# Attention with corner masks by a TensorE product, and small per-row steps on GpSimd

## The chip, the cores and the metric

The kernel runs on one core of a Trainium2 chip. A core has five engines, each with its own instruction queue that is worked off in order: PE (TensorE, matrix products), DVE (VectorE), ACT (ScalarE), POOL (GpSimd) and SP (SyncE, which only issues DMAs here). They wait for one another through semaphores. Products land in PSUM, eight banks of 128 partitions x 2 KB; everything else lies in SBUF. POOL does not read PSUM in this kernel. The metric is the device time of one execution in microseconds.

## The reference

One layer of a streaming encoder, 1024 positions, width 1024. Two groups of 8 heads attend side by side: MLA heads (96 columns for queries and keys, causal in chunks of 64 positions) and band heads (64 columns, each chunk of 64 sees itself and 8 chunks before it, with a bias by relative position). Then one output projection and a gated MLP with a short convolution.

```python
CHUNK = 64; LEFT_CHUNKS = 8; Q_BLOCK = 128
...
q = rmsnorm(q, g_mla_q[l])          # over 96 columns, the 32 rotary ones among them
k = rmsnorm(k, g_mla_k[l])
q = concat([q[..., :NOPE], rope(q[..., NOPE:], positions)])
k = concat([k[..., :NOPE], rope(k[..., NOPE:], positions)])
...
# MLA: blocks of 128 queries
mask = key_chunk[None, :] <= q_chunk[:, None]
p = softmax(where(mask, (q @ k.T) * scale, -1e30))
o_mla = p @ v
...
# band: chunk ci of 64 queries against 576 keys
s = (q @ k.T) * scale + bias
p = softmax(where(kj >= (LEFT_CHUNKS - ci) * CHUNK, s, -1e30))
o_ca = p @ v
...
x = x + g_a * (concat([o_mla, o_ca]) @ w_out)
x = x + g_m * (silu(conv(h @ w_up)[gate]) * conv(h @ w_up)[val]) @ w_down
```

The blocks of 128 queries hold two chunks of 64. In an MLA block, the first 64 queries must not see the last 64 keys: one corner of 64x64 on the diagonal. In a band block from the fifth on, the last 64 queries must not see the first 64 keys: one corner at the other end. The kernel keeps scores negated, so a masked score is +1e30 and the softmax takes a row minimum.

## The kernel before

Values are float32, split into a high and a low part, so that a product is three products on PE (high by high, high by low, low by high). The program is written in Python, and a scheduler with a timeline of its own decides the order of instructions on each engine, by priorities that the code sets and by a few fixed orders (`issue_after`).

The stages, in order of time. First the modulation vectors and the first projections. Then the attention loop at lines 974 to 989: 128 score tiles, 16 units of 4 tiles for the band heads and 16 units of 4 for the MLA heads, in this order. A unit is one head and one half of the queries; a tile is one block of 128 queries. Between the tiles the loop places pieces of other work for PE, the "fillers" (line 924): projections of the next heads (`f_qk`, `f_v`), the latent projection (`f_m`), the MLA up-projections (`f_up`) and the band half of the output projection (`f_oca`). Last come the output projection, the gated MLP and the down-projection, which the change does not touch.

A tile passes through `Unit.scores` (line 735). PE computes its scores into `s`, one of two score areas of 1024 columns in PSUM: line 758 for band tiles, with a stationary page `qh` that holds the query's high part and then `ql` with its low part, line 764 for MLA tiles. DVE writes 1e30 into the 64x64 corner (line 771 for band tiles with `i >= 4`, line 782 for every MLA tile), then takes the row minimum `m` (lines 775 and 779 with the bias, or 783). ACT computes the exponential into `pr` and the row sum `rsum` (line 790), which frees the score area. DVE takes the reciprocal `ri` of the row sum (792) and multiplies it by the constant 2^15 (793). POOL scales the probabilities to a float16 high part (line 73, called at 809), DVE writes the low part (812), and SP issues a transposing DMA (824). The transposed probabilities meet the values on PE three tiles later (`Unit.values`, line 852), and the result is stored by SP (866).

In `f_up` (line 591) each block of 128 positions gives queries and keys of four MLA heads. DVE sums squares (632, 641), adds the sum over the shared rotary part, `ssr`, to the four key sums (642), and POOL makes the reciprocal roots from these (`rsqrt_mean`, lines 117 and 118). DVE then normalises and rotates (648 to 654, with `rope_apply` at 460 to 463). Line 84 is the helper with which POOL or DVE makes the low half of a weight, and line 718 a copy of a query page on POOL.

In tile names, `sc`, `mc`, `Pc`, `hlc`, `ric`, `PTc`, `pvc` belong to band tiles and `sm`, `mm`, `Pm`, `hlm`, `rim`, `PTm`, `pvm` to MLA tiles.

Of the kernel before, what the change touches and what calls it, by code (L numbers as in the profile page):

```python
# [16 lines left out]
BF16 = mybir.dt.bfloat16  # L17
# [7 lines left out]
P = 128  # L25
# [7 lines left out]
BIG = 1e30  # L33
# [31 lines left out]
def layer_kernel(ctx, tc, I, out):  # L65
# [6 lines left out]
    def scale_pool(o, i, s):  # L72
        pool.tensor_scalar(o, i, s, 1.0, op0=MUL, op1=MUL)  # L73
# [25 lines left out]
    make_identity(nc, ident)  # L99
    ones = cst.tile([P, P], F32, name="ones")  # L100
    pool.memset(ones[:], 1.0)
    nhalf = cst.tile([P, 1], F32, name="nhalf")
    pool.memset(nhalf[:], -0.5)
    modT = cst.tile([P, 4, ND], F32, name="modT")
# [486 lines left out]
    def f_up(gr):  # L591
        if gr == 0:
            right.__exit__(None, None, None)
            for i in "4v3":
                G["cm" + i] = tc.tile_pool(name="gp" + i, bufs=1, side="right", reuse_waits="tile")
                G[i] = G["cm" + i].__enter__()
        wq = []
        for k in range(2):
            raw = qtile(f"wqr{gr}_{k}")
            sp.dma_start(raw[:, :384], I["w_qu"][gr][:, k, :])  # L600
            w = g4([P, 2, 512], F32R, f"wq{gr}_{k}")
            hi_of("a", w[:, 0, :384], raw[:, :384])
            lo_of("p", w[:, 1, :384], raw[:, :384], w[:, 0, :384])
            wq.append(w)
        raw = qtile(f"wkr{gr}")
        sp.dma_start(raw[:], I["w_kvu"][gr])
        ssw = cst.tile([P, 1], F32, name=f"sswm{gr}")
        junk = qtile(f"wkj{gr}")
        act.activation(junk[:, 0:256].rearrange("p (a b) -> p a b", a=4),
                       raw[:].rearrange("p (a b) -> p a b", a=4)[:, :, NOPE:], AF.Square, accum_out=ssw[:])  # L610
        vscale["m", gr] = pow2_scale(f"m{gr}", ssw[:], gb2[:], 1, float(KVR))
        sc = vscale["m", gr][0]
        wk = g4([P, 2, 512], F32R, f"wk{gr}")
        hi_of("a", wk[:, 0], raw[:])
        lo_of("p", wk[:, 1], raw[:], wk[:, 0])
        for t in range(NT):
            h, j = divmod(t, 4)
            sl = slice(j * P, (j + 1) * P)
            if t % 2 == 0:
                mq[gr, t // 2] = g3([P, 2, 4, QK], F32, f"qn{gr}_{t}")  # L620
                mk[gr, t // 2] = g3([P, 2, 4, QK], F32, f"kn{gr}_{t}")
                mv[gr, t // 2] = G["v"].tile([P, 2, 4, 2, 64], F16, name=f"vt{gr}_{t}", tag="Gv", bufs=8)
            pt = ps.tile([P, 512], F32, name=f"qu{gr}_{t}", tag="mm", bufs=2)
            yield from gemm3_f(pt[:, :384], [(latT[k, h][:, 0, sl], latT[k, h][:, 1, sl], wq[k][:, 0, :384], wq[k][:, 1, :384])
                                for k in range(2)])
            rq = rtile(f"uqr{gr}_{t}")
            act.activation(rq[:, :384], pt[:, :384], AF.Copy)
            sq = qtile(f"usq{gr}_{t}")
            act.activation(sq[:, :384], rq[:, :384], AF.Square)
            ss = cst.tile([P, 8], F32, name=f"uss{gr}_{t}", tag="ss", bufs=4)  # L630
            r = cst.tile([P, 8], F32, name=f"ur{gr}_{t}", tag="rr", bufs=4)
            dve.tensor_reduce(ss[:, 0:4], sq[:, :384].rearrange("p (a b) -> p a b", a=4), axis=AX.X, op=ADD)
            pt = ps.tile([P, 512], F32, name=f"ku{gr}_{t}", tag="mm", bufs=2)
            yield from gemm3_f(pt[:], [(latT[2, h][:, 0, sl], latT[2, h][:, 1, sl], wk[:, 0], wk[:, 1])])
            p4 = pt[:].rearrange("p (a b) -> p a b", a=4)
            raw = rtile(f"kraw{gr}_{t}")
            r3 = raw[:, :256].rearrange("p (a b) -> p a b", a=4)
            act.activation(r3, p4[:, :, 0:NOPE], AF.Copy)
            s3 = raw[:, 256:512].rearrange("p (a b) -> p a b", a=4)
            act.activation(s3, r3, AF.Square)  # L640
            dve.tensor_reduce(ss[:, 4:8], s3, axis=AX.X, op=ADD)
            dve.tensor_tensor(ss[:, 4:8], ss[:, 4:8], ssr[:, t:t + 1].to_broadcast([P, 4]), op=ADD)
            rsqrt_mean(r[:], ss[:], QK)
            v_t = mv[gr, t // 2][:, t % 2]
            act.activation(v_t[:, :, 0, :], p4[:, :, NOPE:], AF.Copy, scale=sc)
            dve.scalar_tensor_tensor(v_t[:, :, 1, :], p4[:, :, NOPE:], sc, v_t[:, :, 0, :], op0=MUL, op1=SUB)
            q_t = mq[gr, t // 2][:, t % 2]
            dve.tensor_tensor(q_t, rq[:, :384].rearrange("p (a b) -> p a b", a=4),
                              r[:, 0:4].unsqueeze(2).to_broadcast([P, 4, QK]), op=MUL)
            rope_apply(q_t[:, :, NOPE:], q_t[:, :, NOPE:], tabq, t, 4, rq[:, 0:256], dve)  # L650
            k_t = mk[gr, t // 2][:, t % 2]
            dve.tensor_tensor(k_t[:, :, 0:NOPE], r3, r[:, 4:8].unsqueeze(2).to_broadcast([P, 4, NOPE]), op=MUL)
            dve.tensor_tensor(k_t[:, :, NOPE:], kr[:, t:t + 1, :].to_broadcast([P, 4, ROPE]),
                              r[:, 4:8].unsqueeze(2).to_broadcast([P, 4, ROPE]), op=MUL)
# [72 lines left out]
    class Unit:  # L727
# [7 lines left out]
        def scores(u, i):  # L735
# [8 lines left out]
            with tc.high_priority(offset=OFF_S):  # L744
                s = ps.tile([P, 1024], F32, name=f"s{nm}", tag="S", bufs=2)
                n0 = max(0, min(4, i + 1) - lo) * P
                n1 = n - n0
                c0 = 512 - n0 if n1 else 0
                segs = [(c0, lo * P, n0, 0)] if n0 else []
                if n1:  # L750
                    segs.append((512, max(lo, 4) * P - 512, n1, 1))
                q = slice((i % 4) * P, (i % 4 + 1) * P)
                rs_ = slice(u.base, u.base + u.rows)
                if u.band:
                    qh, ql = qpg
                    for a, rr in ((qh[u.odd], slice(0, P)), (ql, rs_)):
                        for c, ko, w, kh in segs:
                            last = pe.matmul(s[:, c:c + w], a[rr, q], kpgs[kh][rr, u.odd, ko:ko + w],
                                             start=(a is not ql), stop=(a is ql))
                else:  # L760
                    for a in range(2):
                        for c, ko, w, kh in segs:
                            for b in range(2 - a):
                                last = pe.matmul(s[:, c:c + w], qpg[a][rs_, q], kpgs[kh][rs_, b, ko:ko + w],  # L764
                                                 start=(a == 0 and b == 0), stop=(a == 1))
                trail.append(last.ins)
                sv = s[:, c0:c0 + n]
                m = cst.tile([P, 1], F32, name=f"m{nm}", tag="m", bufs=4)
                if u.band:
                    if i >= 4:  # L770
                        dve.memset(sv[64:128, 0:64], BIG)
                    w = min(n, 256)
                    if n > 256:
                        m0 = cst.tile([P, 1], F32, name=f"m0{nm}", tag="m0", bufs=4)
                        dve.tensor_reduce(m0[:], sv[:, :n - 256], axis=AX.X, op=MIN)
                        init = m0[:]
                    else:
                        init = 3e38
                    anchor["dve"] = dve.tensor_tensor_reduce(sv[:, n - w:n], sv[:, n - w:n], bias[:, 256 - w:256], 1.0, init,  # L779
                                             ADD, MIN, accum_out=m[:]).ins  # L780
                else:
                    dve.memset(sv[0:64, n - 64:n], BIG)
                    anchor["dve"] = dve.tensor_reduce(m[:], sv, axis=AX.X, op=MIN).ins  # L783
                short = n <= (640 if u.band else 512)
                pieces = [(0, n)] if short else [(0, 512), (512, n)]
                if n <= 640:
                    pr = at.tile([P, 640], F32, name=f"P{nm}", tag="P", bufs=P_BUFS)
                else:
                    pr = pgtile([P, 1024], F32, f"P{nm}")
                act.activation(pr[:, :n], sv, AF.Exp, bias=m[:], scale=-1.0, accum_out=rsum[:, 0:1])  # L790
            with tc.high_priority(offset=OFF_P):
                dve.reciprocal(ri[:], rsum[:, 0:1])
                dve.tensor_scalar(ri[:], ri[:], PSCALE, None, op0=MUL)  # L793
                for x, (p0, p1) in enumerate(pieces):
                    w = p1 - p0
                    cnt[0] += 1
# [773 lines left out]
```

## Time and profile before

| | us |
|---|---|
| runs of the kernel before, median of 3 | 1380.44 (1379.88 to 1385.12) |
| the profiled execution, own time | 1379.88 |
| its span, first to last instruction | 1378.1 |
| first and last start of band score products (line 758) | 92.8 to 377.3 |
| first and last start of MLA score products (line 764) | 413.8 to 633.0 |
| last product of probabilities and values (line 852), start | 647.1 |
| first product of the MLP (line 1068), start | 734.6 |
| mean granted clock of PE | 0.940 |

How to read the views that follow. In a view of stretches each engine's column gives its busy microseconds and, in brackets, its instructions; then come the clock granted to PE (1 is full), the mean busy share of the DMA engines, and GB/s. In a list of waits, "A L1 <- B L2: t, n, m" says that A's instructions of line 1 began late because of B's of line 2, t us in total, n times, m us at most. A group of instructions has its line, engine and operation, output and input tiles with their shapes, its count, busy us, the mean of one in ns, and the idle time before it. A line of one source gives shortest/median/longest in ns. A timeline starts with the start and the duration in us. Instructions on one engine overlap a little in the records, so that durations add up to more than the time from start to start.

### The profile page before, as it was taken

What the parts mean: (1) busy time and instruction counts of PE and PEld (TensorE: products, weight loads), DVE (VectorE), ACT (ScalarE), POOL (GpSimd) and SP (SyncE); (2) the same over time, 40 slices, a digit from 0 to 9 for tenths busy, and PEclk for the clock granted to TensorE, in tenths of its full rate; (3) what the DMA queues carried; (4) which work ended last, traced back from release to release, by engine and by line L of the source; (5) the groups of instructions that cost most, each with busy time, mean ns of one, the idle gap of its engine ahead of it and who ended that gap; (6) DMA issues with size and microseconds to landing.
All of it is one profiled execution on the core that took longest, in us unless ns stands there. A gap on an engine that the chain in (4) does not pass through costs nothing.

```text
span 1378.1 us, 18696 instructions
## 1 busy us (share of the span) xinstructions
PE 1229.5 (89%) x6168; PEld 1009.3 (73%) x6168; DVE 1105.8 (80%) x1928; ACT 622.0 (45%) x1131; POOL 572.2 (42%) x610
## 2 busy tenths in 40 slices
PE   4889698989867779886997999999999999999998
PEld 3788487977655567674775888777788888888886
DVE  6957878676589997885689689898988888688667
ACT  4443445444455554554365443434444444443341
POOL 5454556365646574343643443434444442200000
PEclk9999797999787989997998999999999999999999
DMA  8314557666322468678921233333323224983451
GB/s 321 129 41 91 135 144 189 157 137 146 64 50 74 81 141 183 136 136 204 376 101 46 87 128 104 121 128 116 109 92 113 92 100 142 340 308 119 130 161 61
DMA packets 223689, 190.57 MB, mean 138 GB/s; under 512 B 148708, under 2 KB 166884, under 8 KB 223592
## 3 DMA queue, kind: packets, MB, share of 16 engines
q1 hardware_dynamic: 223592, 189.38, 47.5%
q8 instruction: 48, 0.79, 0.2%
q14 instruction: 49, 0.40, 0.1%
HBM read 117.24 MB, written 37.49 MB: 112 GB/s over the span
## 4 chain that ended last, share of the span: by engine, by line
PE 44%; DVE 16%; issue 5%; ACT 4%; DMA 4%; POOL 2%; SPq 0%; ACTq 0%; DVEq 0%; POOLq 0%
PE p L1068 6%; PE p L1070 6%; PE p L1069 6%; PE dnA_P L1381 2%; PE dnA_P L1383 2%; PE dnA_P L1382 2%; PE sm L764 2%; DVE u L1235 2%; PE dnB_P L1383 1%; PE dnB_P L1381 1%; PE dnB_P L1382 1%; DMA adaw<-w_ada 1%; DVE hlm L812 1%; DVE u L1234 1%; PE pvm L852 1%
## 5 line engine op out<-in xcount | busy, mean ns | idle before, releaser
L77 ACT ACTIVATE dnP<-dnr 128x1024 fp32r<-128x1024 f32 x73 | 77.4, 1062 | 113.1 <-PE dnA_P L1383 46.4
L1355 DVE TENSOR_TENSOR dnP<-dnr,dnP 128x1024 fp32r<-128x1024 f32 x72 | 89.5, 1246 | 46.5 <-ACT dnP L77 46.5
L73 POOL TENSOR_SCALAR hlm<-Pm,rim 128x512 f16<-128x512 f32 (+3 forms) x96 | 66.6, 702 | 75.8 <-ACT Pm L790 21.2
L1234 DVE SCALAR_TENSOR_TENSOR u<-c,cvp,u 128x1023 f32<-128x1023 f32 x44 | 62.0, 1449 | 29.6 <-ACT u L1233 29.6
L84 POOL TENSOR_TENSOR wf<-wu,wf 128x512 fp32r<-128x512 f32 x22 | 35.8, 1628 | 118.5 <-ACT wf L77 118.5
L73 POOL TENSOR_SCALAR hlc<-Pc,ric 128x640 f16<-128x640 f32 (+2 forms) x64 | 47.4, 744 | 72.2 <-DVE ric L793 40.6
L812 DVE SCALAR_TENSOR_TENSOR hlm<-Pm,rim,hlm 128x512 f16<-128x512 f32 (+3 forms) x96 | 67.7, 714 | 8.8 <-POOL hlm L73 8.4
L790 ACT ACTIVATE Pm<-sm,mm 128x128 f32<-128x128 f32 (+3 forms) x64 | 47.2, 738 | 52.5 <-DVE mm L783 31.8
L84 POOL TENSOR_TENSOR wb<-wu,wb 128x512 fp32r<-128x512 f32 x22 | 38.8, 1763 | 73.1 <-ACT wb L77 72.1
L1233 ACT ACTIVATE u<-c,cvp 128x1024 f32<-128x1024 f32 x44 | 52.3, 1237 | 34.4 <-DVE c L1304 25.8
L1235 DVE SCALAR_TENSOR_TENSOR u<-c,cvp,u 128x1022 f32<-128x1022 f32 x44 | 64.8, 1512 | 0.0
L852 PE MATMUL pvm<-PTm,vt 128*128 128x256 f16 (+1 forms) x320 | 45.9, 295 | 20.9 <-DMA PTm<-hlm 13.9
L790 ACT ACTIVATE Pc<-sc,mc 128x640 f32<-128x640 f32 (+2 forms) x64 | 42.0, 657 | 48.5 <-DVE mc L779 35.8
L812 DVE SCALAR_TENSOR_TENSOR hlc<-Pc,ric,hlc 128x640 f16<-128x640 f32 (+2 forms) x64 | 53.5, 840 | 12.7 <-POOL hlc L73 12.5
L852 PEld LDWEIGHTS <-vt 128*128 128x128 f16 x320 | 31.9, 109 | 35.7 <-DMA PTm<-hlm 14.4
L154 PE MATMUL ipq<-wq_s,hT 128*128 128x256 f32 x192 | 55.9, 294 | 1.2 <-ACT wq_s L77 1.2
L155 PE MATMUL ipq<-wq_s,hT 128*128 128x256 f32 x192 | 56.4, 294 | 0.1
L156 PE MATMUL ipq<-wq_s,hT 128*128 128x256 f32 x192 | 56.0, 292 | 0.0
L77 ACT ACTIVATE wc<-ws 128x512 fp32r<-128x512 f32 x21 | 13.3, 632 | 93.6 <-DVE ws L1087 93.6
L1382 PE MATMUL dnA_P<-dnP 128*128 128x512 f32 x132 | 51.3, 389 | 0.0
L1383 PE MATMUL dnA_P<-dnP 128*128 128x512 f32 x132 | 51.3, 389 | 0.0
L1381 PE MATMUL dnA_P<-dnP 128*128 128x512 f32 x132 | 51.2, 389 | 0.0
(432 smaller groups left out, 4453.4 us busy)
## 6 DMA issues: line engine op xcount, KB each, us to landing
wu<-w_up SPq DMA_DIRECT2D x44, 512.0 KB, 3.8
dnr<-g_d SPq DMA_DIRECT2D x73, 256.0 KB, 4.4
aw<-w_ada SPq DMA_DIRECT2D x48, 256.0 KB, 3.5
g_d<-u SPq DMA_DIRECT2D x22, 512.0 KB, 2.8
dnr<-w_down SPq DMA_DIRECT2D x44, 256.0 KB, 5.6
adaw<-w_ada_a SPq DMA_DIRECT2D x16, 512.0 KB, 6.1
x<-x SPq DMA_DIRECT2D x16, 512.0 KB, 9.0
g_d<-gs SPq DMA_DIRECT2D x22, 256.0 KB, 2.2
```

What stands on the lines that cost most here:

```text
L73: pool.tensor_scalar(o, i, s, 1.0, op0=MUL, op1=MUL)
L77: act.activation(o, i, AF.Copy)
L790: act.activation(pr[:, :n], sv, AF.Exp, bias=m[:], scale=-1.0, accum_out=rsum[:, 0:1])
L812: dve.scalar_tensor_tensor(hl[:, w:2 * w], pp, ri[:], hl[:, :w], op0=MUL, op1=SUB)
L852: last = pe.matmul(dst, u.vst(j), mov, start=(x == 0), stop=(x == len(todo) - 1), skip_group_check=True)
L1068: pe.matmul(pt, sh, pg[:, 0], start=(k == 0 and not add), stop=False, skip_group_check=skip)
L1069: pe.matmul(pt, sh, pg[:, 1], start=False, stop=False, skip_group_check=skip)
L1235: dve.scalar_tensor_tensor(u[:, 2:], c[:, :S - 2], cvp[:, cv:cv + 1], u[:, 2:], op0=MUL, op1=ADD)
L1355: r = f(*a, **k)
L1381: pe.matmul(pt, sh, w[:, 0, 0], start=start, stop=False, skip_group_check=add)
L1382: pe.matmul(pt, sh, w[:, 1, 0], start=False, stop=False, skip_group_check=add)
L1383: pe.matmul(pt, sl, w[:, 0, 0], start=False, stop=stop, skip_group_check=add)
```

## The change

Three edits. The corner masks are no longer written by DVE: between the products with the high and the low part of the queries, PE adds a product of one row. Its stationary is one partition of a constant tile, 64 zeros and 64 times 1e30 (or the reverse), its moving operand 64 ones, and its output the 64 columns of the corner on all 128 queries, so that 1e30 is added to 64 queries and zero to the others. The multiplication of the reciprocal row sums by 2^15 goes from DVE to POOL, by the helper that POOL uses for the probabilities. The addition of the rotary sums of squares to the key sums goes from DVE to POOL. Two constant tiles are made by POOL at the start.

```diff
+    mones = cst.tile([P, 64], BF16, name="mones")
+    pool.memset(mones[:], 1.0)
+    mrow = cst.tile([P, 3, 64], BF16, name="mrow")
+    pool.memset(mrow[:], 0.0)
+    pool.memset(mrow[:, 1], BIG)
+    mflat = mrow[:].rearrange("p a b -> p (a b)")
...
-            dve.tensor_tensor(ss[:, 4:8], ss[:, 4:8], ssr[:, t:t + 1].to_broadcast([P, 4]), op=ADD)
+            pool.tensor_tensor(ss[:, 4:8], ss[:, 4:8], ssr[:, t:t + 1].to_broadcast([P, 4]), op=ADD)
...
                     for a, rr in ((qh[u.odd], slice(0, P)), (ql, rs_)):
+                        if i >= 4 and a is ql:
+                            pe.matmul(s[:, c0:c0 + 64], mflat[0:1, 0:P], mones[0:1], start=False, stop=False,
+                                      skip_group_check=True)
                         for c, ko, w, kh in segs:
...
                     for a in range(2):
+                        if a:
+                            e = segs[-1][0] + segs[-1][2]
+                            pe.matmul(s[:, e - 64:e], mflat[0:1, 64:64 + P], mones[0:1], start=False, stop=False,
+                                      skip_group_check=True)
                         for c, ko, w, kh in segs:
...
-                    if i >= 4:
-                        dve.memset(sv[64:128, 0:64], BIG)
...
-                    dve.memset(sv[0:64, n - 64:n], BIG)
...
                 dve.reciprocal(ri[:], rsum[:, 0:1])
-                dve.tensor_scalar(ri[:], ri[:], PSCALE, None, op0=MUL)
+                scale_pool(ri[:], ri[:], PSCALE)
```

The helper that it calls stood in the kernel before:

```python
    def scale_pool(o, i, s):
        pool.tensor_scalar(o, i, s, 1.0, op0=MUL, op1=MUL)
```

The scheduler lays out the attention stages anew with these instructions; from the early part of the MLP on the order is that of before.

## The prediction

> **What bounds the kernel now.** I read the page's engine line first, then the stretches of the span, then the waits, then single lines.
>
> ```profile
> span 1378.1 us, 18696 instructions
> PE 1229.5 (89%) x6168; PEld 1009.3 (73%) x6168; DVE 1105.8 (80%) x1928; ACT 622.0 (45%) x1131; POOL 572.2 (42%) x610
> ```
>
> PE is the busiest engine of the whole span, but that is an average over stages. The change touches only instructions that run between the first score product and the last softmax, so the next view cuts the span there: band attention (92 to 392 us), the MLA up-projection (392 to 416), MLA attention beside the second up-projection (416 to 500), MLA attention beside part of the output projection (500 to 640), and the rest.
>
> ```profile
> core 0: us, PE busy (x) PEld busy (x) DVE busy (x) ACT busy (x) POOL busy (x), PEclk, DMA share, GB/s
> 92.00:392.00 300.00, 264.17 (x1634) 222.88 (x1635) 220.29 (x613) 136.42 (x348) 159.84 (x233) 0.89 0.56 128
> 392.00:416.00 24.00, 16.36 (x77) 11.38 (x74) 21.11 (x68) 14.55 (x34) 11.56 (x11) 1.00 0.06 15
> 416.00:500.00 84.00, 59.88 (x273) 46.30 (x274) 77.93 (x231) 46.98 (x112) 57.55 (x58) 0.76 0.41 93
> 500.00:640.00 140.00, 122.15 (x693) 96.93 (x693) 116.23 (x285) 69.68 (x146) 61.44 (x83) 0.96 0.74 150
> 640.00:1378.00 738.00, 703.64 (x3067) 574.24 (x3065) 601.24 (x597) 313.60 (x420) 228.91 (x160) 0.97 0.41 144
> ```
>
> Dividing busy by length: in the band stage PE leads (88%, DVE 73%); from 392 to 500 DVE leads (21.11+77.93 of 108, 92%, PE 71%); from 500 to 640 the two are level (PE 87%, DVE 83%). POOL is nowhere above 69%. So the change, which moves work from DVE to PE and POOL, meets three different limits. Which wait ends last there:
>
> ```profile
> POOL hlc L73 <- DVE ric L793: 40.6, 13, 7.5
> ACT Pm L790 <- DVE mm L783: 31.8, 17, 4.2
> POOL uss L117 <- DVE uss L642: 29.7, 11, 5.2
> POOL hlm L73 <- DVE rim L793: 12.0, 8, 2.7
>   ACT Pm L790: 24.4, 24
> ```
>
> The columns are total us, times, longest. The last row is of line 764: PE stood idle 24.4 us before MLA score products until an exponential had emptied one of the two score banks. The exponential itself waits for DVE's row minimum (L783), and POOL's probability scaling (L73) waits for DVE's scaled reciprocal (L793). The loop is PE scores, DVE minimum, ACT exponential, PE scores; DVE's queue is what is late in it.
>
> **What is removed.** Counting instructions in the program: 32+64 memsets of a 64x64 corner (L771, L782), 128 one-column scalings (L793), 16 four-column additions (L642); 240 DVE instructions.
>
> ```profile
> L771 DVE MEMSET sc<- x32: 112/112/112, 124.4 to 378.1; 64x64 f32 x32
> L782 DVE MEMSET sm<- x64: 112/112/112, 416.1 to 633.5; 64x64 f32 x64
> L793 DVE TENSOR_SCALAR rim<-rim x64: 125/142/155, 418.0 to 637.8; 128x1 f32<-128x1 f32 x64
> ```
>
> By stretch (us busy, count), first L782, then L793, then L642:
>
> ```profile
> 416.00:500.00 84.00, 2.20 (x20) 0.76 0.41 93
> 500.00:640.00 140.00, 4.89 (x44) 0.96 0.74 150
> ...
> 92.00:392.00 300.00, 9.22 (x64) 0.89 0.56 128
> 416.00:500.00 84.00, 2.65 (x19) 0.76 0.41 93
> 500.00:640.00 140.00, 6.55 (x45) 0.96 0.74 150
> ...
> 392.00:416.00 24.00, 0.86 (x6) 1.00 0.06 15
> 416.00:500.00 84.00, 1.76 (x10) 0.76 0.41 93
> ```
>
> From 392 to 500, where DVE leads, 2.20+2.65+0.86+1.76 = 7.5 us leave its queue; I count all of it. From 500 to 640, 4.89+6.55 = 11.4 us leave; PE is just as full, so I count half, 5.7. In the band stage 32x0.112+9.22 = 12.8 us leave an engine that is not the limit; I count nothing, and would count a third (4.3) if DVE set the pace there too. Bounds: 0 and the whole 31.7.
>
> **What PE gets.** 96 products of a one-row stationary (128 columns, bf16) with 64 moving columns, each with a weight load, put between the high and the low score products. No row shows such a product. The nearest is eight load-and-multiply pairs with one moving column:
>
> ```profile
> 270.28 0.95 PE L436 MATMUL p_ada<-ones,aacc 128*128 128x1 f32 x8
> 271.09 0.36 PE L154 MATMUL ipq<-wq_s,hT 128*128 128x256 f32 x1
> ```
>
> Eight pairs take 271.09-270.28 = 0.81 us, 0.10 each; a short product cannot cover the load that follows it, so the pair costs a load whatever its width. I take 0.10 (bounds 0, if the loads hide behind the 512-column products beside it, and 0.20, if the next load is bared as well). Band: 32x0.10 = 3.2 us on the leading engine, counted whole. 416 to 500: 20x0.10 = 2.0 us beside a fuller DVE, counted as nothing; without that cover it is 2.0. 500 to 640: 44x0.10 = 4.4, half counted, 2.2. The product reads only constants, so it adds no wait; what is queued behind it is the low product that ends the tile. The memset's 0.112 us between scores and minimum goes, PE's 0.10 comes, so a tile's own latency stays.
>
> **What POOL gets.** 128 one-column scalings, 16 four-column additions, three memsets at the start. Nearest rows:
>
> ```profile
> L483 POOL TENSOR_SCALAR mss<-mss 128x1 f32<-128x1 f32 x8 | 2.1, 267 | 0.7
> L117 POOL TENSOR_SCALAR uss<-uss 128x8 f32<-128x8 f32 x16 | 5.7, 353 | 30.8 <-DVE uss L642 29.7 <-DVE rim L793 0.8
> L118 POOL TENSOR_TENSOR rx<-ssx,nhalf x8: 549/549/868, 12.8 to 23.2; 128x1 f32<-128x1 f32 x8
> ```
>
> A scaling is taken at 0.27 us: 128x0.27 = 34.6 us on an engine that is busy 159.84+11.56+57.55+61.44 = 290.4 of the 548 us from 92 to 640. The additions lie inside the 29.7 us for which POOL waited for DVE's addition; with the cover gone they cost 16x0.35 = 5.6. POOL's first use of a sum is at 12.8 us, after its start-up memsets. The handover of one tile, with DVE's queue empty and with something in it:
>
> ```profile
> 582.53 0.17 DVE L792 RECIPROCAL rim<-rsm 128x1 f32<-128x1 f32 x1
> 582.73 0.15 DVE L793 TENSOR_SCALAR rim<-rim 128x1 f32<-128x1 f32 x1
> 583.04 1.04 POOL L73 TENSOR_SCALAR hlm<-Pm,rim 128x512 f16<-128x512 f32 x2 [3.30 <-ACT Pm L790]
> ...
> 576.22 0.16 DVE L792 RECIPROCAL rim<-rsm 128x1 f32<-128x1 f32 x1
> 576.30 0.67 DVE L783 TENSOR_REDUCE mm<-sm 128x1 f32<-128x512 f32 x1
> 576.89 0.14 DVE L793 TENSOR_SCALAR rim<-rim 128x1 f32<-128x1 f32 x1
> 577.28 0.59 POOL L73 TENSOR_SCALAR hlm<-Pm,rim 128x384 f16<-128x384 f32 x1 [0.43 <-DVE rim L793]
> ```
>
> From the reciprocal's start to POOL's first work on the probabilities: 0.51 us and 1.06 us. With the scaling on POOL it would be 0.17 + a handover of 0.16 (582.88 to 583.04) + 0.27 = 0.60. So a tile that met a queue gains 0.46 and one that did not loses 0.09. POOL waited for the scaling in 13+8 = 21 tiles of 128: 21x0.46 = 9.7 gained, 107x0.09 = 9.6 lost. I take 0 (bounds -9.7 and 128x0.09 = +11.5). The new wait is POOL's for the reciprocal. In the changed order 75 of the 128 scalings stand directly ahead of their own tile's L73; behind the other 53 stand low halves of weights (L84), query copies (L718) and powers (L118), which PE's fillers, the score products and the next norms wait for.
>
> POOL's additional instructions can also hold up DVE:
>
> ```profile
> 427.71 2.62 POOL L84 TENSOR_TENSOR wo<-wor,wo 128x512 fp32r<-128x512 f32 x2
> 428.02 1.17 DVE L462 TENSOR_TENSOR qn<-uqr 128x64 f32<-128x64 f32 x1
> 429.12 1.29 DVE L463 TENSOR_TENSOR qn<-uqr 128x64 f32<-128x64 f32 x1
> ...
> L462 DVE TENSOR_TENSOR qn<-uqr 128x64 f32<-128x64 f32 x1 | 0.2, 203 | 0.0
> L812 DVE SCALAR_TENSOR_TENSOR hlm<-Pm,rim,hlm 128x512 f16<-128x512 f32 (+3 forms) x96 | 67.7, 714 | 8.8 <-POOL hlm L73 8.4
> ```
>
> A DVE subtraction of two SBUF tiles that takes 0.203 us alone took 1.17 and 1.29 beside two POOL subtractions. L812 is such an instruction and fills 67.7 of 224 us, 30%. A 0.27 us scaling that falls on one holds it for 0.13 us on average: 64x0.30x0.13 = 2.5 us in the MLA stages and less in the band stage; I take 2 (bounds 0 and 144x0.27 = 39). The Trainium skill, "SBUF — State Buffer", section "Who interferes with whom", says more: VectorE with two SBUF inputs and a GpSimd instruction that reads SBUF exclude each other, and the later one is blocked for the other's whole length. The 1.29 us row agrees. By that rule each POOL scaling is bought with its full length whenever it meets such an instruction, which is the first rival.
>
> **The sum.** -7.5 -5.7 +2.2 +3.2 +0 +2 = -5.8 us, against the profiled execution's own 1379.88 us (span 1378.1 and 1.8 around it): 1374.1, so 1374. The median of the three runs, 1380.44, lies 0.6 above that execution, within what runs differ by.
>
> One thing is in no term: instructions are laid out anew. Outside the longest common order, 897 of PE's 6739 instructions, 418 of DVE's 1691 that remain, 166 of 956 on ACT, 89 of 616 on POOL and 101 of 685 on SP stand elsewhere, most of them in the attention stages and the last early in the MLP; on SP that puts probability transposes and stores of attention outputs ahead of or behind loads of weights. It can go either way by several us, and widens the range by 6.
>
> **Rivals.**
> *POOL's scalings hold DVE* (slower). For: the row of 1.29 us, and L812 following each scaling closely. Against: the scaling is short, and DVE's minima (0.67 us at 576.30) read a score bank and only one operand. Price: every scaling and addition blocks DVE for 0.27 us. From 392 to 500, (19+16)x0.27 = 9.5 whole; from 500 to 640, 45x0.27 = 12.2, half, 6.1. In place of the 2 that gives -5.8-2+15.6 = +7.8: 1388. It decides from the point where the average block exceeds what the scaling freed, 0.14 us. The skill's page on SBUF, named above, states this rival's rule.
> *DVE sets the pace throughout* (larger gain). For: the first four rows of the waits. Against: 88% PE in the band stage. -7.5-11.4-4.3, PE only in the band stage, +3.2: -20, 1360.
> *The change frees nothing that counts.* The loop waits on transposes of the probabilities and on score banks, and DVE only idles longer. Against: 92% from 392 to 500. Then only the additions' 0.86+1.76 gain and PE's 3.2 are paid: 1380.5.
>
> **How the numbers follow.** Forecast 0.40 (own range 1368 to 1380, half of it below 1373.5), larger gain 0.22 (1360), nothing 0.10 (1380.5), POOL holds DVE 0.28 (1388). A measurement of this kernel can tell about 0.5%, 6.9 us, from no change. Faster: 0.20+0.22 = 0.42; within: 0.20+0.10 = 0.30; slower: 0.28. Range: 1360, the larger gain, to 1394, the slower rival with the 6 of the new order.
>
> **What would show it.** DVE busy down by about 30 us, all between 92 and 640; POOL up by about 35 to 40. L73's waits for the reciprocal well under the 40.6+12.0 of before. The mask products 0.1 us apart from their neighbours, PE's busy time up by 10 to 20. The stretch from 392 to the last softmax shorter by some 9 us, the band stage longer by 3; after it both programs alike. Wrong if L812 and L648 grow in mean by more than 0.1 us (first rival), if the band stage moves by more than 8 us either way (the new order), or if a mask product takes 0.2 us or more.

## The result and the profile after

| | us |
|---|---|
| changed kernel, median of 16 runs | 1387.01 (1379.06 to 1394.89) |
| kernel before, median of 16 runs beside them | 1379.70 (1374.86 to 1385.12) |
| ratio, 95% interval | 1.0055 (1.0035 to 1.0074) |
| profiled execution of the changed kernel, own time | 1393.37, span 1391.6 |

The change makes the kernel slower by about 7.6 us. 1374 and a gain were forecast: the time lies inside the range, the direction was wrong. The profiled execution took 6.4 us more than the median, so its stretches are to be read for shape and not to the microsecond. The engine line of the page after:

```profile
span 1391.6 us, 18773 instructions
PE 1260.4 (91%) x6264; PEld 1026.4 (74%) x6264; DVE 1086.8 (78%) x1688; ACT 621.3 (45%) x1131; POOL 615.3 (44%) x757
```

DVE lost 240 instructions but only 19.0 us of busy time, POOL gained 43.1 us and PE 30.9. The stretches, cut near the same events as before (first band score, last band values, first MLA score, start of the output projection's pieces, 7 us ahead of the last MLA values); the columns are those of before:

```profile
95.80:396.30 300.50, 268.34 (x1661) 227.98 (x1662) 207.31 (x511) 134.76 (x344) 175.38 (x295) 0.89 0.56 128
396.30:421.00 24.70, 16.58 (x74) 12.63 (x72) 21.21 (x63) 15.44 (x37) 13.94 (x19) 0.93 0.05 14
421.00:510.40 89.40, 75.75 (x330) 55.05 (x329) 82.11 (x197) 50.06 (x118) 69.13 (x96) 0.74 0.45 100
510.40:655.50 145.10, 133.34 (x718) 99.33 (x715) 102.55 (x187) 69.07 (x144) 73.10 (x119) 0.94 0.68 143
```

The band stage is as long as before (300.5 us). In the last stretch PE is now at 133.34/145.1 = 92% and DVE at 71%, where 87% and 83% stood before: the two are no longer level. The waits of the loop:

```profile
POOL ric L73 <- DVE ric L802: 61.0, 24, 8.3
POOL rim L73 <- DVE rim L802: 47.3, 26, 6.6
ACT Pm L800 <- DVE mm L793: 27.3, 25, 3.7
DVE mm L793 <- PE sm L777: 20.2, 21, 2.6
POOL uss L648 <- DVE uss L647: 19.8, 10, 6.0
```

Lines after the edits are 6 to 13 higher than before: 802 is the reciprocal, 793 the MLA row minimum, 777 the MLA score products, 822 the low part. POOL stands 108.3 us before its new scalings. The fourth row has grown too: DVE's minimum waits 20.2 us for PE's scores, where before it was the memset that met the scores first and waited 6.4 us. The mask products themselves, weight load and product of line 773:

```profile
L773 PEld LDWEIGHTS <-mrow x64: 90/91/100, 423.2 to 647.3; 1*128 1x128 bf16 x64
L773 PE MATMUL sm<-mones,mrow x64: 188/198/232, 423.2 to 647.3; 1*128 1x64 bf16 x64
  issue: 12.1, 34
```

The product's record is 0.198 us long. The weight unit idles 12.1 us before 34 of the loads with nothing to wait for, and a load starts 0.004 us ahead of its product (median of the 64), where the loads of the MLA high products start 0.22 us ahead: the mask rows are not loaded ahead.

### The profile page after: what moved, and what is told of

Same layout as the page of the kernel before. It is cut to its first block, busy times and chain, and to the rows that moved or that the text cites. A ratio compares the mean times of both kernels' runs of the same rounds, so it can differ in the third digit from the quotient of the medians.

```text
span 1391.6 us, 18773 instructions
## 1 busy us (share of the span) xinstructions
PE 1260.4 (91%) x6264; PEld 1026.4 (74%) x6264; DVE 1086.8 (78%) x1688; ACT 621.3 (45%) x1131; POOL 615.3 (44%) x757
## 4 chain that ended last, share of the span: by engine, by line
PE 52%; DVE 19%; DMA 9%; POOL 7%; issue 7%; ACT 5%; SPq 1%; POOLq 0%; DVEq 0%; ACTq 0%
PE p L1080 5%; PE p L1078 5%; PE p L1079 5%; PE sm L777 3%; PE sc L767 2%; DVE u L1245 2%; PE dnA_P L1391 2%; PE dnA_P L1393 2%; PE dnA_P L1392 2%; DMA PTm<-hlm 2%; DVE u L1244 2%; DMA adaw<-w_ada 2%; PE pvm L862 1%; PE dnB_P L1392 1%; PE dnB_P L1393 1%
## 5 line engine op out<-in xcount | busy, mean ns | idle before, releaser
L73 POOL TENSOR_SCALAR hlm<-Pm,rim 128x512 f16<-128x512 f32 (+2 forms) x96 | 69.5, 731 | 15.7 <-DMA PTm<-hlm 11.6
L822 DVE SCALAR_TENSOR_TENSOR hlm<-Pm,rim,hlm 128x512 f16<-128x512 f32 (+2 forms) x96 | 69.3, 736 | 8.9 <-POOL hlm L73 8.7
L793 DVE TENSOR_REDUCE mm<-sm 128x1 f32<-128x128 f32 (+3 forms) x64 | 47.5, 749 | 20.4 <-PE sm L777 20.2
L161 PE MATMUL ipq<-wq_s,hT 128*128 128x256 f32 x192 | 57.6, 300 | 0.0
L160 PE MATMUL ipq<-wq_s,hT 128*128 128x256 f32 x192 | 57.1, 299 | 0.0
L162 PE MATMUL ipq<-wq_s,hT 128*128 128x256 f32 x192 | 56.9, 297 | 0.0
```

The lines of the kernel that those rows point to most:

```text
L822: dve.scalar_tensor_tensor(hl[:, w:2 * w], pp, ri[:], hl[:, :w], op0=MUL, op1=SUB)
```

## The experiments

Each ratio is to runs of the kernel before on the same chip, with its 95% interval; "us" beside it is (ratio - 1) x 1380. Theory M: a mask product costs PE about 0.2 us where PE sets the end. Theory H: POOL's place in the reciprocal's path costs. Theory V: VectorE's relief decides. Theory O: the new order of the instructions decides.

**Each edit in the order that the scheduler makes of it.** `e1_mask` has the masks alone:

```diff
-                        dve.memset(sv[64:128, 0:64], BIG)
-                    dve.memset(sv[0:64, n - 64:n], BIG)
+                            pe.matmul(s[:, c0:c0 + 64], mflat[0:1, 0:P], mones[0:1], ...)
+                            pe.matmul(s[:, e - 64:e], mflat[0:1, 64:64 + P], mones[0:1], ...)
```

> The masks alone: 96 one-row products on TensorE in place of 96 memsets on VectorE; scaling and additions stay on VectorE. Theory M (each product costs TensorE about 0.2 us, since its 0.09 us weight load stands bare and the next load too, in stages where TensorE is the leading or second engine): 96x0.2 = 19 us of TensorE more, half of it on the path, less some 5 us that VectorE gives back: +4 to +10 us against before, PE busy +17 to +22. Theory H (the handover of the reciprocal to POOL is what costs): -3 to +1 us, since nothing of it is in this kernel. Theory O (the new order of the instructions costs, whatever the edit): anything within 8 us either way, with the low-rank stage ordered as in the changed kernel.

1.0044 (1.0021 to 1.0067), +6 us. `e4_scale_sums` has the other two edits:

```diff
-                dve.tensor_scalar(ri[:], ri[:], PSCALE, None, op0=MUL)
+                scale_pool(ri[:], ri[:], PSCALE)
-            dve.tensor_tensor(ss[:, 4:8], ss[:, 4:8], ...)
+            pool.tensor_tensor(ss[:, 4:8], ss[:, 4:8], ...)
```

> The scalings and the additions on POOL, the corners still by memsets of VectorE: 144 instructions less on VectorE, 144 more on POOL, no mask product. Theory M: -4 to 0 us against before, as the prediction's VectorE terms without its TensorE terms. Theory H (POOL stands in its queue for a reciprocal, 108 us in the changed kernel against 53 us for the scaling before, and then runs late; or POOL's reads hold VectorE): +5 to +8 us, the whole of the changed kernel's loss. Theory O: within 8 us either way.

0.9918 (0.9891 to 0.9946), -11 us: faster than both kernels. Its waits:

```profile
POOL ric L73 <- DVE ric L792: 66.4, 26, 8.2
POOL rim L73 <- DVE rim L792: 55.0, 31, 3.9
```

POOL waits longer for reciprocals here (121.4 us) than in the changed kernel (108.3) and the kernel is the fastest of all. Theory H, by which this wait is the loss, falls.

`a_free` is the kernel before without memsets and without masks, `a_pay` the one with its memsets and 96 products of zeros besides:

```diff
 a_free
-                        dve.memset(sv[64:128, 0:64], BIG)
-                    dve.memset(sv[0:64, n - 64:n], BIG)
 a_pay
-    pool.memset(mrow[:, 1], BIG)
+                        dve.memset(sv[64:128, 0:64], BIG)
+                    dve.memset(sv[0:64, n - 64:n], BIG)
```

The second part of the diff is against `e1_mask`: its masks are zeros and the memsets are back.

> Before without its 96 corner memsets and without any mask in their place (left out: the masking of the corners of the scores). This is the gain of taking the memsets from VectorE with nothing paid on TensorE. Theory M: -6 to -3 us (96x0.112 = 10.8 us of VectorE busy time, of which the 32 in the band stage lie beside a leading TensorE). If it is near 0, the memsets were hidden and the masks could only lose. Theory O: within 8 us either way.

> Before with its memsets kept and 96 one-row products of zeros added on TensorE: the price of the product without any gain (nothing is computed otherwise). Theory M: +8 to +16 us, 96x0.2 = 19 us of TensorE busy time of which half or more shows, and e1_mask lies at the sum of this and of the kernel without masks. With 0.1 us a product, as predicted, +4 to +5 us. Theory H: 0 to +3. Theory O: within 8 us either way, with no relation to the other two mask kernels.

`a_free`: 1.0002 (0.9981 to 1.0023), 0 us. `a_pay`: 1.0132 (1.0104 to 1.0160), +18 us. Their sum, +18, isn't the +6 of the masks alone: numbers of single edits do not add.

`e2_scale` and `e3_sums` halve `e4_scale_sums`; `e7_band` and `e8_mla` add to it the 32 band masks or the 64 MLA masks.

```diff
 e2_scale
+                scale_pool(ri[:], ri[:], PSCALE)
 e3_sums
+            pool.tensor_tensor(ss[:, 4:8], ss[:, 4:8], ...)
 e7_band, to e4_scale_sums
+                            pe.matmul(s[:, c0:c0 + 64], mflat[0:1, 0:P], mones[0:1], ...)
-                        dve.memset(sv[64:128, 0:64], BIG)
 e8_mla, to e4_scale_sums
+                            pe.matmul(s[:, e - 64:e], mflat[0:1, 64:64 + P], mones[0:1], ...)
-                    dve.memset(sv[0:64, n - 64:n], BIG)
```

> The 128 scalings of the reciprocal on POOL, nothing else of the change. Scalings and additions together had brought 0.9918 of before, -11 us. Theory V (VectorE's queue is what the scalings free: 128 instructions less in the queue that the scores' minimum and the low parts stand in): most of it, -10 to -6 us, with a 512-column low part (L812) shorter than before's 706 ns and the row of the reciprocal waiting less. Theory O (the order of the instructions after 300 us differs and that decides): anything within 8 us, with no relation to the two parts' sum. Theory H: 0 to +5.

> The 16 additions of the rotary square sums on POOL, nothing else of the change. Theory V: -4 to 0 us, since only 16 instructions leave VectorE, in the stretch where it leads (400 to 500 us), and a short addition there waits in a full queue. Theory O: within 8 us either way; -6 or below, or +4 or above, would show that the order of the instructions alone moves as much as the whole change.

> Scalings and additions on POOL, and the 32 mask products of the band stage; the 64 corners of the low-rank stage stay with VectorE's memsets. Theory M, against the kernel with scalings and additions alone (0.9918 of before, 1371 us): a product in its place measured about 0.2 us from the last high product to the first low one, so 32x0.2 = +6 us, all in the band stage: 1376 to 1379, 0.995 to 0.998 of before. The prediction's price would give +3. Theory O: no relation to the number of products.

> Scalings and additions on POOL, and the 64 mask products of the low-rank stage; the 32 corners of the band stage stay with VectorE's memsets. Theory M, against the kernel with scalings and additions alone (1371 us): 64x0.16 to 64x0.24 = +10 to +15 us, all in the low-rank stage: 1380 to 1386, 0.999 to 1.004 of before. The prediction's price would give +2. Together with the band's 32 it should make up the changed kernel's +16 over the kernel without products. Theory O: no such sum.

`e2_scale`: 0.9939 (0.9914 to 0.9963), -8 us. `e3_sums`: 1.0099 (1.0076 to 1.0123), +14 us, from 16 additions that together take 2.8 us on VectorE. `e7_band`: 1.0026 (1.0010 to 1.0041), +4; `e8_mla`: 0.9980 (0.9960 to 1.0000), -3. The 32 products cost 15 us over `e4_scale_sums` and the 64 cost 9, so no price per product fits. Theory O had named +4 or more for `e3_sums` as its mark.

**The same edits with the order held.** The order in which the scheduler had put the kernel before's instructions was written down for each engine's queue, SyncE's DMA issues among them, and given to the variant as edges between neighbours, which order the issue and add no wait:

```diff
+    for e, packed in ORDER.items():
...
+        for a, b in zip(order[:-1], order[1:]):
+            tc.add_manual_dep(lists[e][b], lists[e][a].name, mybir.DependencyInfo(
+                mybir.DependencyClass.NoSync, mybir.DependencyReason.DATA), reason="order")
```

`p_after` has the whole change in the order of before, `p_ss` scalings and additions, `p_mask` the masks, `p_pay` products of zeros with the memsets kept. `q4_before` is the reverse: the instructions of the kernel before, in the order of `e4_scale_sums`.

> The whole change, but every engine's instructions and SyncE's DMA issues held in the order that they have in the kernel before (edges between neighbours of one queue, which add no wait); what is added stands right ahead of the instruction that it is written ahead of, what is removed leaves no gap. Theory O (the new order that the scheduler made of the change is what costs): -8 to 0 us against before, as the prediction's sum without its new order. Theory M (mask products cost about 0.2 us of TensorE each, and outweigh what VectorE gives back, in any order): +4 to +12 us.

> Scalings and additions on POOL, in the order of the kernel before: TensorE's, ScalarE's and SyncE's queues are the same, instruction for instruction. In its own order this edit gave 0.9918, -11 us, and the additions alone in theirs +12. Theory O: -2 to +2 us, both were the order. Theory V (VectorE's relief by 144 short instructions is the gain): -11 to -5. Theory H (the handover holds): +2 to +8.

> The masks alone, in the order of the kernel before: 96 mask products, each right ahead of its tile's first low product, 96 memsets less. Theory M: +6 to +16 us (from the last high product to the first low one 0.40 us with the product, 0.18 and 0.29 without it, so 0.1 to 0.22 each). Theory O: -4 to +3 us, the +6 of the masks alone was their order. By the prediction's terms: -1.

> The kernel before with its memsets kept and 96 one-row products of zeros, in the order of before. In its own order this cost +18 us. By the prediction's 0.10 us a product, with half and all of it on the path in its two stages: +5 us. By 0.1 to 0.22 us each, from the time between the last high and the first low product: +10 to +18. If the +18 were the order: 0 to +4.

> The kernel before's own instructions (scalings and additions on VectorE, memsets) in the order of the kernel with scalings and additions on POOL, which took 0.9918. Theory O: all of that gain is the order, so -13 to -8 us. Theory V: the order gives nothing and the relief does: -2 to +2 us.

| edits | own order | order of before | order of `e4_scale_sums` |
|---|---|---|---|
| none | 1 | 1 | 0.9948 (0.9925 to 0.9971) |
| scalings, additions | 0.9918 (0.9891 to 0.9946) | 0.9957 (0.9936 to 0.9978) | the own one |
| masks | 1.0044 (1.0021 to 1.0067) | 0.9983 (0.9958 to 1.0009) | not tried |
| products of zeros, memsets kept | 1.0132 (1.0104 to 1.0160) | 1.0049 (1.0027 to 1.0072) | not tried |
| all three | 1.0055 (1.0035 to 1.0074) | 1.0006 (0.9982 to 1.0030) | 1.0006 (0.9984 to 1.0029) |

Down the second and the third column only the edits differ (in the first the order changes with them), along a row only the order. The row of all three: the same instructions take 1.0055 in the order the scheduler made and 1.0006 in the order of before. The row of none: the same instructions gain 7 us from another order alone. So of the 11 us of `e4_scale_sums` some 5 to 7 us are its order and 4 to 6 the edits: `p_ss` at -6 lies in the range of theory V, `q4_before` at -7 between the ranges of O and V. The changed kernel's loss against before is its order; `p_after` at +0.8 lies between the ranges of O (-8 to 0) and M (+4 to +12).

What the masks do is read down the second column. Alone they come to -2 us: the products cost +7 (`p_pay`), so leaving the memsets out gave 9 back. On top of the scalings and additions they cost 1.0006 - 0.9957, +7 us; if the products cost 7 there too, leaving the memsets out gives nothing more. The same tile shape, two high products and a low one of 384 columns, first without (`p_ss`) and then with the mask (`p_after`), starts and durations in us:

```profile
515.15 0.52 PE L764 MATMUL sm<-mk,mq_0h 96*128 96x384 f32 x2
515.51 0.34 PE L764 MATMUL sm<-mk,mq_0l 96*128 96x384 f32 x1
```

```profile
565.79 0.51 PE L777 MATMUL sm<-mk,mq_0h 96*128 96x384 f32 x2
566.24 0.20 PE L773 MATMUL sm<-mones,mrow 1*128 1x64 bf16 x1
566.37 0.44 PE L777 MATMUL sm<-mk,mq_0l 96*128 96x384 f32 x1
```

From the first high product to the low one 0.36 us and 0.58 us: in its place a product costs 0.22 us, three times what reaches the end (7/96 = 0.07). Over all 64 MLA tiles the median from the start of the last high product to that of the first low one is 0.17 us in the trace of before and 0.40 in that of `p_after`. The engine line and the last MLA stretch of `p_ss`, then of `p_after`:

```profile
PE 1225.2 (89%) x6168; PEld 1004.9 (73%) x6168; DVE 1088.4 (79%) x1784; ACT 621.1 (45%) x1131; POOL 613.0 (45%) x754
500.00:638.50 138.50, 117.78 (x669) 92.27 (x668) 105.91 (x225) 67.58 (x140) 70.08 (x123) 0.94 0.77 156
```

```profile
PE 1244.9 (91%) x6264; PEld 1013.5 (74%) x6264; DVE 1086.9 (79%) x1688; ACT 621.9 (45%) x1131; POOL 612.7 (45%) x757
500.00:641.30 141.30, 128.69 (x727) 96.50 (x725) 101.45 (x185) 68.63 (x143) 69.70 (x123) 0.97 0.77 155
```

In the MLA stretch the masks raise PE from 117.78/138.5 = 85% to 91%, and lower DVE from 76% to 72%. PE leads there before the masks come. That fits time given to DVE being worth nothing there and time taken on PE being paid, but no run leaves the memsets out on top of the scalings and additions without adding the products, so it is argued and not shown.

`q4_after` is the whole change in the order of `e4_scale_sums`, `q3_before` the kernel before in the order of `e3_sums`.

> The whole change in the order of the kernel with scalings and additions alone (0.9918 with them, 0.9948 with none of the edits). If order and edits add up: the order's -7 us and the edits' +0.7 us, so 0.993 to 0.998 of before. If the masks cost about 0.2 us each on TensorE here: 0.9918 plus 10 to 16 us, 0.999 to 1.004.

> The kernel before's own instructions in the order of the kernel with the additions alone on POOL, which took 1.0099. Theory O (order alone): +9 to +14 us, 1.0065 to 1.010. If the additions on POOL cost by themselves: -2 to +3 us.

`q4_after`: 1.0006 (0.9984 to 1.0029), 12 us over `e4_scale_sums` in the same order, so the masks cost there too, more than the +7 in the order of before (the intervals overlap). That is inside the range given for 0.2 us a product and outside the one for edits and order that add up. `q3_before`: 1.0066 (1.0043 to 1.0088): +9 of the +14 us of the additions are an order; the rest is at the edge of what the intervals can tell.

**What in the new order costs.** In the changed kernel the products of 24 of 128 score tiles stand in turns with those of another tile on TensorE, against 12 in the order of before, and DVE waits 20.2 us for MLA scores, where `p_after` has this row among its waits from 386 to 665 us:

```profile
DVE mm L793 <- PE sm L777: 5.5, 11, 1.1
```

`qa_deint` keeps all queues of the changed kernel and puts 57 products so that the first tile's come first:

```diff
- sm_4 hi, sm_5 hi, sm_4 mask, sm_5 mask, sm_4 lo, sm_5 lo, sm_4 lo, sm_5 lo
+ sm_4 hi, sm_4 mask, sm_4 lo, sm_4 lo, sm_5 hi, sm_5 mask, sm_5 lo, sm_5 lo
```

> The changed kernel in its own order, except that 57 products of score tiles stand elsewhere in TensorE's queue: wherever products of two score tiles follow one another in turns with nothing else between, all of the first tile's come first. Alternating tiles fall from 24 to 16, all other queues are the same. Theory I (the turns make both tiles late, and VectorE waits for the first tile's end, 20.2 us in the low-rank stage against 5.5 in the order of before): the wait of the row minimum for the scores falls to 6 to 12 us and the time by 4 to 8 us, to 0.999 to 1.003 of before. Theory R (the rest of the order is what costs): the wait falls and the time stays at 1.004 to 1.007.

1.0085 (1.0058 to 1.0112), no gain, and the wait is still there, in the list of waits of the span:

```profile
ACT Pm L800 <- DVE mm L793: 30.6, 22, 4.1
DVE mm L793 <- PE sm L777: 19.6, 20, 2.1
```

Taking out these 57 turns lowered neither the wait, which both theories had expected to fall, nor the time, so they are not what costs; the 16 tiles that still alternate were not tried. The last two hold only a part of the queues in the order of before: `r_pe` TensorE's, `r_rest` the other four.

```diff
 r_pe
+ORDER = {"PE": ...}
 r_rest
+ORDER = {"DVE": ..., "Activation": ..., "Pool": ..., "SP": ...}
```

> The whole change, TensorE's queue alone held in the order of before; VectorE, ScalarE, POOL and SyncE as the scheduler sets them around it (as far from the order of before as in the changed kernel: on VectorE 1160 lines of difference, on SyncE 358). If TensorE's order carries the loss: 0.998 to 1.003 of before. If the order of the other queues does: 1.003 to 1.008.

> The whole change, the queues of VectorE, ScalarE, POOL and SyncE held in the order of before, TensorE's as the scheduler sets it (1417 lines of difference from the order of before, about half of the changed kernel's). If TensorE's order carries the loss: 1.003 to 1.008 of before. If the order of the other queues does: 0.998 to 1.003.

`r_pe`: 1.0041 (1.0023 to 1.0060), +6 us. `r_rest`: 1.0003 (0.9982 to 1.0025), 0 us. With TensorE's queue as before there is still a loss, with the other four as before there is none. That points to the four and does not prove it: the queues left free were laid out anew in both kernels, so neither has the changed kernel's own. The two profiled executions lie the other way round from the medians (`r_pe` 1378.35 us against a median of 1383.65, `r_rest` 1383.73 against 1378.80), so their waits show a shape and not the loss. Two of them, first in `r_pe`, then in `r_rest`:

```profile
DVE mm L793 <- PE sm L777: 13.5, 17, 2.0
POOL ric L73 <- DVE ric L802: 66.1, 25, 9.8
```

```profile
DVE mm L793 <- PE sm L777: 8.0, 11, 1.4
POOL ric L73 <- DVE ric L802: 48.3, 20, 8.0
```

DVE's wait for MLA scores is 5.5 and 8.0 us in the two without a loss and 13.5, 19.6 and 20.2 in the three with one, but `e4_scale_sums` has 12.9 us of it at its memsets and is faster than before, so it is not shown to be the cause.

**Where the time lies.** One row from the last band values to the last MLA values, and one from the first product of the MLP to the end; first the changed kernel, then `p_after`. (The MLP's first product writes `c_g`, at 701.5 us in the trace of before; the 734.6 of the table of before is a later tile's.)

```profile
396.30:662.50 266.20, 228.93 (x1133) 169.27 (x1130) 206.87 (x446) 134.97 (x299) 156.17 (x232) 0.86 0.55 118
721.10:1391.60 670.50, 647.99 (x2837) 530.36 (x2836) 566.59 (x566) 291.64 (x384) 197.79 (x132) 0.99 0.38 129
```

```profile
385.80:641.00 255.20, 217.93 (x1127) 161.43 (x1124) 204.29 (x440) 131.97 (x292) 154.85 (x231) 0.90 0.59 120
698.90:1373.10 674.20, 649.93 (x2838) 531.81 (x2836) 564.31 (x566) 292.28 (x384) 195.62 (x132) 0.98 0.37 128
```

In these two executions the MLA stage is 11 us longer in the new order and the MLP, which no edit touches, 4 us shorter. The second holds in the other traces: the MLP takes 674 to 677 us in the six kernels with the four queues of before (before itself, the four `p_` kernels, `r_rest`) and 667 to 672 in 13 of the 14 others (`e8_mla` 676). So the new orders gain a few us behind the attention, and by these traces the changed kernel loses more inside it than shows at the end. `r_pe` loses elsewhere: its MLA stage takes 255 us in its trace, its band stage 305.

The granted clock goes along with these times. PE's 6264 products, the same in both, are busy 1260.4 us in the changed kernel's trace (clock 0.935) and 1244.9 in `p_after`'s (0.946). Over the 35 executions of the kernel before that ran beside `p_after`, 0.01 less clock goes with about 10 us more (correlation -0.75; 3 to 10 us in the other groups). The mean clock over all executions is 0.942 in the changed kernel, 0.945 in `p_after`, 0.939 in `r_pe` and 0.946 in `r_rest`. By these slopes, as an estimate, 1 to 3 of the 6.8 us between the first two go with the clock, and 2 to 8 us, as much as the 5 that they differ by, between the last two. Whether a lower clock is the way in which an order costs, or only its companion, no run separates. Which queues carry the loss, and by which instructions, stays open.

## Why the prediction was wrong

The step that failed is the one the prediction put in no term: "instructions are laid out anew", taken as nothing with 6 us either way. The edits as such, in the order of before, took 1.0006, +0.8 us (-2.5 to +4.1); the order that the scheduler made of them added the other 6.8 (1.0055 against 1.0006; by the two intervals 3 to 11). That is about the 6 us that the range allowed for it, and it is what made the kernel slower than before. In which queues it arises stays open; `r_pe` and `r_rest` point to those of VectorE, ScalarE, POOL and SyncE.

The sum itself was a second miss of the same size: -5.8 us against +0.8. Point by point:

- **Scalings and additions.** By the prediction's terms 2.65+0.86+1.76 whole, half of 6.55, and +2 for blocking: -6.5. Held to the order of before they gave -6 (-9 to -3). The number is right, in part by luck: the traces show no blocking of DVE (below), and DVE's cover shrinks by much less than these records.
- **Masks.** By its terms -2.2-2.4+2.2+3.2 = +0.8. Held: -2 (-6 to +1). The number is right, and so is the price on the end, 5.4 us against the 7 (4 to 10) of `p_pay`, but by luck: the product takes 0.22 us in its place, not 0.10 (the case that the prediction gave as its upper bound, with the next load bared as well), and a third of it shows, not half or all. By the prediction's own test the product's record of 0.198 us stood at the edge of "wrong".
- **Adding them.** Together they came to +0.8, not to -8 (-2 and -6, with an interval of about 5 either way). The prediction counted half of each microsecond that left DVE from 500 to 640, whichever edit took it. The rows of `p_ss` fit that the first edit used up this slack, PE leading at 85% against 76%, and that the masks then only cost; this is argued and not shown.
- **The durations.** The removed records add up to 32.2 us, and DVE's busy time fell by 18.9 (`p_after`). In the trace of before, DVE's records without these 240 cover 15.8 us less: a one-column operation lies partly under its neighbour, as the rows quoted in the prediction show (a minimum of 0.67 us from 576.30, a scaling that starts at 576.89, before it ends). From 392 to 500 the cover shrinks by 2.2 us, not 7.5, and from 500 to 640 by 7.0, not 11.4. With these the prediction's sum is -2.2-3.5+2.2+3.2+2 = +1.7, close to the measured +0.8, but the single edits do not bear it out: by cover the masks alone would be -0.9-1.5+2.2+3.2 = +3.0, where -2 (-6 to +1) was measured. So the sum of the records is not what DVE gains, and the cover is not shown to be it either.
- **The handover**, taken as nothing: right for the time, wrong in its sign on the page. POOL's wait for reciprocals rose from 52.6 us to 108.3 instead of falling well under it, and `e4_scale_sums`, with 121.4 us of it, gained 11 us.
- **POOL's scalings hold DVE**, the rival whose time (1388) came closest: not the cause. Its mark was a growth by over 0.1 us of the mean of the low part (822, before 812) or of the queries' normalisation (654, before 648). The changed kernel:

```profile
L822 DVE SCALAR_TENSOR_TENSOR hlm<-Pm,rim,hlm 128x512 f16<-128x512 f32 (+2 forms) x96 | 69.3, 736 | 8.9 <-POOL hlm L73 8.7
L654 DVE TENSOR_TENSOR qn<-uqr,ur 128x384 f32<-128x384 f32 x16 | 10.1, 631 | 1.4 <-POOL ur L124 1.2
```

736 ns after 714 and 631 after 671, and the edit that carries all of these scalings gained 6 us with the order held. Where the two meet in the trace, it is the scaling that waits. A low part with the scaling beside it, and the MLA scalings as a group, in the changed kernel:

```profile
584.77 0.75 DVE L822 SCALAR_TENSOR_TENSOR hlm<-Pm,rim,hlm 128x512 f16<-128x512 f32 x1
584.94 0.63 POOL L73 TENSOR_SCALAR rim<-rim 128x1 f32<-128x1 f32 x1 [2.78 <-DVE rim L802]
L73 POOL TENSOR_SCALAR rim<-rim x64: 182/191/1212, 428.9 to 653.7; 128x1 f32<-128x1 f32 x64
```

The scaling starts inside the low part and ends 0.05 us after it, in 0.63 us in place of the median 0.19. Of all 128 scalings, 36 take over 0.25 us, 14.2 us more together, and 34 of these end within 0.1 us after a DVE instruction beside them. The low part is not longer for it: the four of 512 columns that met a scaling and no other POOL instruction took 0.734 us in the mean, the 17 that met no POOL instruction 0.746. By the Trainium skill, "SBUF — State Buffer", section "Who interferes with whom", a VectorE instruction with two SBUF inputs and a GpSimd instruction that reads SBUF contend for an exclusive lock. The trace agrees with that; the rival had the wrong one of the two waiting, and its +7.8 us rest on that. What POOL's waiting costs at the end, no run separates.

- **The marks in the profile.** DVE fell by 19.0 us, not 30; POOL rose by 43.1, near the 35 to 40; PE by 30.9, more than 10 to 20, but 15.4 in `p_after` with the same products at a higher clock. From the end of the band stage to the last MLA values it took 255 us before (392 to 647.1), 266 in the changed kernel (396.3 to 662.5) and 255 in `p_after` (386.0 to 641.3), not 9 less. One profiled execution each, and executions of one kernel differ by several us.
- **DVE sets the pace throughout** (1360) and **frees nothing that counts** (1380.5): the first falls with the 92% of PE in the last stretch. The second gives the time of `p_after`, 1379.4, by another way: not that nothing is freed, but that the masks spend it. The 1388 of the rival above is luck in the same way.

Single edits in their own order misled as long as they were read as prices: `e1_mask` +6 and `a_pay` +18 looked like theory M with 0.2 us a product, and became -2 and +7 when the order was held.

## To carry to other kernels

Where a scheduler lays out the queues, an edit has two effects, its own and that of the order that it draws; here two other orders of the very same instructions took 7 us less and 9 us more, and with the order of before held no edit was worth more than 7 us. Before an edit is judged, hold the order of the queues and measure it there, and look for a better order separately. Do not price removed short operations by the sum of their records: here 32.2 us of records covered only 15.8 us that no neighbour covered. Count the same idle time for one edit only; that the masks came to -2 us alone and to +7 on top of the scalings and additions suggests it. And read the granted clock beside every time.

## What the runs showed of the hardware

A bf16 product of one row and 64 columns between fp32r products of 384 columns delayed the next by 0.22 us: its load of 0.09 us starts together with it and is not done ahead, though the constant has been there since the start, as another tile of `p_after` shows. The load of the low product behind it, which starts 0.22 us ahead in the trace of before (median), starts 0.002 us ahead in that of `p_after`.

```profile
561.25 0.20 PE L773 MATMUL sm<-mones,mrow 1*128 1x64 bf16 x1
```

```profile
561.25 0.09 PEld L773 LDWEIGHTS <-mrow 1*128 1x128 bf16 x1
```

A one-column POOL operation of 0.19 us that meets a VectorE instruction with two SBUF inputs can last until that one ends: 0.63 us beside a low part of 0.75. And edges of order alone, on four queues (`r_rest`, 1.0003, against 1.0055 in the scheduler's order), were worth 7 us of 1380 in a kernel whose busiest engine stands at 91%.
